# A decoder step whose first stage takes its input rows feature-major from the host: no transposes of x, and priority for the readers of the w_in products

## The chip, the cores and the metric

The kernel runs on one core of a Trainium2 chip. The metric is the device time of one execution in microseconds; the median of several runs counts. A core has five engines with a queue each: TensorE (PE, matmuls; PEld is its weight load), VectorE (DVE), ScalarE (ACT), GpSimd (POOL) and SyncE (SP), which in this kernel issues nearly all transfers.

## The reference

One inference step of a hybrid decoder layer, in float32, for a prompt of 2048 positions and a group of 8 × 8 sample positions, 1024 features:

```python
h = rmsnorm(x, g_pre_mix)
q, k, v, u = split(h @ w_in)        # 512 + 128 + 128 + 512 columns
attn = sink_attention(rope(q), rope(k), v)   # 8 heads, 2 kv heads, head_dim 64, window 128
pool = pool_mix(u)                  # trailing means over 2/4/8/16 positions, per-group map
x += rmsnorm(concat(rmsnorm(attn), rmsnorm(pool)) @ w_out)
x += rmsnorm(relu(rmsnorm(x) @ w_up)**2 @ w_down)
x += sigmoid(x @ w_ple_gate + b) * (p @ w_ple)
```

Outputs are y of both groups and the new key, value and pooling states.

## The kernel before

A product in float32 accuracy is done by `mm3` as three matmuls over values split in two: `hi` (a cast to a rounded format) and `lo` (the rest, computed by `lo_of` on VectorE). L129, L130 and L131 of the profile are these three; L125 is `lo_of`, wherever it is called from.

The program has several stages; the change lies in the first, the attention stage, up to the first matmul of w_out (its tile is `pab`, L129 and L130 in the profile), which starts at 443.44 us. After it come w_out, the two matrices of the feed-forward part (by a Strassen scheme) and the gate.

The attention stage walks over tiles of 128 positions: tile −1 is the sample (64 rows), 0 to 15 the prompt. For a tile t:

- `head(t)` issues the load of the rows `x` and of the rotary table `cs` on SP, and computes the rows' norm: ScalarE squares x into `junk` with an accumulated sum (L223), the small `rstd_of` follows, and VectorE scales `cs` with it.
- `front(t)` transposes x on TensorE in two groups of four (tile `trh`, L236, in PSUM), splits each group into `hT` (ScalarE casts, L237; VectorE subtracts, L125), and multiplies by w_in (tiles `wi`, resident in SBUF) into three PSUM tiles: `kvps` (keys and values, 24 matmuls of 256 columns), `qps` (24 of 512) and `ups` (24 of 512). The three share the two banks of the pool `mmp`. `rope` reads kvps and qps on VectorE (L258, twice L261) and adds on GpSimd (L262); the values go to `vp` (a ring of three) by two ScalarE operations and one on VectorE (L283 to L285); u goes to SBUF by ScalarE (L326). q and k are split (`qhl`, `khl`) and transposed again (`trq`, `trk`) into `qT` and `kp`. These transposes, trh and those of the attention share the two banks of the pool `tr`.
- `attention(t)`: scores `sc` (L357, L358), a fused mask and maximum on VectorE (L361, `nm`), the exponential on ScalarE (L372), the sink terms `es`, the scaling of `pr` (L387 on ScalarE, L389 on VectorE), transposes of it (`trp`, L399), their split `pt` (L401, L125), the product with the values `po` (L409, L410), and `mix` (L412, L413). `pooling(t)` works on u (L434 to L479) and has the matmuls `pq`; `finish(t)` sums squares (`pss`) and stores mix by SP to DRAM (`mixd`, L494).

The Python generators of one iteration are woven in the order that a string of letters gives (`ORDER`; f is front(t+1), a attention(t), p pooling(t), l the last finish), and the framework's scheduler then sets the order of each engine's instructions for the whole program, with each engine taking its own strictly in that order. Loads that go through `queue` keep the program's order on SP.

Towards the end of the stage w_out is loaded, and split on ScalarE (L761) and VectorE (L762) into `wo`.

Of the kernel before, what the change touches and what calls it, by code (L numbers as in the profile page):

```python
# [22 lines left out]
NS = NDEC * TDEC  # L23
# [9 lines left out]
NT = SEQ // P  # L33
# [7 lines left out]
C_HOT = C_ICNT + 64  # L41
C_COLS = C_HOT + 4

ORDER = "f f a f f l f f a f p p a f f f f a p a f f f l f a f f f"

ORDER1 = "f f f a f f f l f f a f f a f p f f f f p l f a a p a"
ORDER0 = "a f a p a p f f a a f a f a f a f p f f"


UP_N = 352  # L50
# [2 lines left out]
def tn(t):  # L53
    return NS if t < 0 else P
# [32 lines left out]
def trunk(ctx: ExitStack, tc: tile.TileContext, i: dict, o: dict):  # L87
    nc = tc.nc
    V, A, G, T, SY = nc.vector, nc.scalar, nc.gpsimd, nc.tensor, nc.sync

    xp = i["x_prompt"][0]
    xs = i["x_sample"].rearrange("b t d -> (b t) d")
    p_t = i["p_t"].rearrange("(k p) t -> p k t", p=P)
    w_in, w_out, w_up, w_down = (i[n][0] for n in ("w_in", "w_out", "w_up", "w_down"))
    w_ple, w_gate = i["w_ple"][0], i["w_ple_gate"][0]
# [3 lines left out]
    def xrows(t):  # L99
        return xs if t < 0 else xp[t * P : (t + 1) * P]  # L100
# [4 lines left out]
    ident = cp.tile([P, P], F32, name="ident")  # L105
# [14 lines left out]
    def queue(out, in_):  # L120

        tc.keep_in_program_order(SY.dma_start(out, in_))

    def lo_of(out, full, hi, eng=V):
        eng.tensor_tensor(out=out, in0=full, in1=hi.bitcast(F32), op=ALU.subtract)  # L125
# [7 lines left out]
    def rstd_of(pool, ss, n, dim, cols=1):  # L133

        r = pool.tile([P, cols], F32, tag="rst", bufs=6, name="rst")
        G.tensor_scalar(out=r[:n], in0=ss, scalar1=1.0 / dim, scalar2=EPS, op0=ALU.mult, op1=ALU.add)  # L136
        q = pool.tile([P, cols], F32, tag="rsq", bufs=6, name="rsq")
        G.tensor_tensor(out=q[:n], in0=r[:n], in1=mhalf[:n].to_broadcast([n, cols]) if cols > 1 else mhalf[:n], op=ALU.pow)
        return q


    with ExitStack() as sa:
        wp = sa.enter_context(tc.tile_pool(name="wp", bufs=1))
        fp = sa.enter_context(tc.tile_pool(name="fp", bufs=2))
# [4 lines left out]
        tr = sa.enter_context(tc.tile_pool(name="tr", bufs=2, space=PSUM))  # L149
        op = sa.enter_context(tc.tile_pool(name="op", bufs=2, space=PSUM))  # L150
# [62 lines left out]
        def head(t):  # L213

            n = tn(t)
            x = fp.tile([P, D], F32, tag="x", bufs=2, name="x")
            queue(x[:n], xrows(t))
            cs = fp.tile([P, 128], F32, tag="cs", bufs=2, name="cs")
            r0 = SEQ if t < 0 else t * P
            queue(cs[:n], i["rope"][r0 : r0 + n])  # L220
            junk = fp.tile([P, D], BF16, tag="rb", bufs=2, name="junk")
            ss = pa.tile([P, 1], F32, tag="ss", bufs=3, name="ss")
            A.activation(out=junk[:n], in_=x[:n], func=AF.Square, accum_out=ss[:n])  # L223
            rs = rstd_of(pa, ss[:n], n, D)
            V.tensor_scalar_mul(cs[:n], cs[:n], rs[:n])
            return x, cs, rs

        def front(t, x, cs, rs, res):
            n = tn(t)
            hTs = []  # L230
            for j in range(2):
                hT = fp.tile([P, 2, 4, P], F32R, tag="hT", bufs=4, name="hT")
                hTs.append(hT)
                ps = tr.tile([P, 4, P], F32, tag="tr", name="trh")
                for c in range(4):
                    T.transpose(ps[:, c, :n], x[:n, (j * 4 + c) * P : (j * 4 + c + 1) * P], ident[:n, :n])  # L236
                A.copy(out=hT[:, 0, :, :n], in_=ps[:, :, :n])  # L237
                lo_of(hT[:, 1, :, :n], ps[:, :, :n], hT[:, 0, :, :n])
                yield

            def gemm(c0, cw, ps, step=2):
                for k in range(8):
                    if k and k % step == 0:
                        yield
                    mm3(
                        ps[:n, :cw],
                        (hTs[k // 4][:, 0, k % 4, :n], hTs[k // 4][:, 1, k % 4, :n]),
                        (wi[k][:, 0, c0 : c0 + cw], wi[k][:, 1, c0 : c0 + cw]),
                        k == 0,
                        k == 7,  # L250
                    )

            def rope(ps, h, out):

                s = ps.rearrange("p (h d) -> p h d", h=h)
                b = fp.tile([P, 8, HD], F32, tag="rb", bufs=2, name="rb")[:n, :h]
                cc = cs[:n, 0:64].unsqueeze(1).to_broadcast([n, h, 64])
                V.tensor_tensor(out=out, in0=s, in1=cc, op=ALU.mult)  # L258
                for u in range(2):
                    sn = cs[:n, 64 + u * 32 : 96 + u * 32].unsqueeze(1).to_broadcast([n, h, 32])  # L260
                    V.tensor_tensor(out=b[:, :, u * 32 : u * 32 + 32], in0=s[:, :, (1 - u) * 32 : (1 - u) * 32 + 32], in1=sn, op=ALU.mult)  # L261
# [16 lines left out]
            if t >= 0:  # L278
                vp = vps[t % 3]
                vv = kvps[:, 128:256].rearrange("p (g d) -> p g d", g=2)  # L280

                hi = vp[:, 0:6].rearrange("p (a b) d -> p b a d", b=3)[:, 0]
                A.mul(out=hi, in_=vv, mul=rs)  # L283
                A.mul(out=vp[:, 4:8].rearrange("p (a b) d -> p b a d", b=2)[:, 0], in_=vv, mul=rs)
                V.scalar_tensor_tensor(out=vp[:, 1:3], in0=vv, scalar=rs, in1=hi.bitcast(F32), op0=ALU.mult, op1=ALU.subtract)  # L285
            yield
            if t >= 0:
                qps = mmp.tile([P, 512], F32, tag="mm", name="qps")
# [13 lines left out]
            if t >= 0:  # L302
                ups = mmp.tile([P, 512], F32, tag="mm", name="ups")
            for j, _ in enumerate(gemm(768, 512, ups) if t >= 0 else ()):
                yield
                if j == 0:
                    kp = over.pool.tile([P, 4, 256], F32R, tag="kp", bufs=2, name="kp")
                    ps = tr.tile([P, 4, P], F32R, tag="tr", name="trk")
# [8 lines left out]
                if j == 2:  # L317
                    qT = over.pool.tile([P, NH, P], F32R, tag="qT", bufs=1, name="qT")
                    for j in range(2):
                        ps = tr.tile([P, 4, P], F32R, tag="tr", name="trq")  # L320
# [2 lines left out]
                        A.copy(out=qT[:, 4 * j : 4 * j + 4, :], in_=ps.bitcast(F32))  # L323
                    yield
            u = pa.tile([P, 512], F32, tag="u", bufs=2, name="u")
            A.mul(out=u[:n], in_=ups[:n], mul=rs[:n])  # L326
# [4 lines left out]
            if t < 0:  # L331
                for src, dst, c in (
# [4 lines left out]
                    d = dp.tile([NS, c], F32, name="fresh")  # L337
# [261 lines left out]
        def run(*gens):  # L599
            for g in gens:  # L600
                for _ in g:
                    pass

        def weave(order, **gens):
            for c in order.split():
                next(gens[c], None)
            run(*gens.values())

        heads = {-1: head(-1)}
        load_gains(["g_pre_mix"], 0)  # L610
        for k in range(8):
            load_w_in(k)
# [33 lines left out]
    with ExitStack() as sb:  # L646
# [95 lines left out]
        with ExitStack() as s2:  # L742
# [106 lines left out]
            for tp in [0, 1, -1, 2, 3, 4, 5, 6]:  # L849
                h = []  # L850
# [543 lines left out]
```

## Time and profile before

| | |
|---|---|
| runs | 2210.32, 2214.53, 2217.34 us (median 2214.53) |
| profiled execution | 2212.33 us, its span 2210.5 us, mean granted clock 0.989 |
| PE busy, whole span | 2151.4 us (97%) |
| DVE, ACT, POOL busy | 1579.4, 957.8, 566.4 us |
| attention stage | 0 to 443.44 us |
| first kvps matmul of two tiles in steady state | 174.82 and 198.31 us |
| trh matmuls of the prompt, sum of their durations | 128 × 276 ns on average |
| `hT` casts of the prompt on ACT, subtractions on DVE | 32 × 581 ns, 32 × 685 ns |

Times are microseconds from the first instruction. In rows with starts, the first number is the start and the second the duration. A matmul's duration runs from its start to its modelled end and overlaps with the next one's; the distance between starts tells what it takes of the engine. In rows of groups the numbers behind the bar are the sum of busy time, the mean in ns, and the idle time of the engine just before them with what ended it. A row of waits gives who waited for whom, the total, how often, and the longest.

### The profile page before, as it was taken

To read this page: it belongs to the slowest core of one execution; us is meant where nothing else is said; L and a number is where in the kernel's file an instruction comes from. 1 tells how busy PE (TensorE), PEld (TensorE's weight loads), DVE (VectorE), ACT (ScalarE), POOL (GpSimd) and SP (SyncE) were. 2 spreads that over 40 slices of the span, in tenths; PEclk is the share of its full clock that TensorE was granted. 3 is DMA by queue.
4 is the path that set the end of the run, shared out by engine and by line. 5 is a ranking of instruction groups with operands and counts; after the bars stand their busy time and mean duration, and the time that the engine had idled before them with its cause. 6 is when DMAs were issued, how large, how long until landed. Compare 5 with 4: busy or idle time off the path is not lost. (4 is left out here: it accounts for less than half of the span.)

```text
span 2210.5 us, 31375 instructions
## 1 busy us (share of the span) xinstructions
PE 2151.4 (97%) x11571; PEld 1899.4 (86%) x11571; DVE 1579.4 (71%) x2716; ACT 957.8 (43%) x1856; POOL 566.4 (26%) x641
## 2 busy tenths in 40 slices
PE   8999999699989999999999999999999999999999
PEld 6888888588878999999999988788888888877887
DVE  5788888756688777655755565888888888866553
ACT  4656666634455445444644454332233232222221
POOL 2343433224340000000000045535535544300000
PEclk9999999799999999999999999999999999999999
DMA  5111110456789767766676642222321222143211
GB/s 204 51 42 43 60 43 32 135 170 194 231 249 328 238 207 256 235 193 194 204 220 197 187 122 67 89 79 68 98 89 58 89 97 85 61 150 95 82 58 39
DMA packets 288306, 295.01 MB, mean 133 GB/s; under 512 B 77654, under 2 KB 239650, under 8 KB 281977
## 3 DMA queue, kind: packets, MB, share of 16 engines
q1 hardware_dynamic: 288153, 293.01, 42.5%
q8 instruction: 91, 1.49, 0.3%
q14 instruction: 62, 0.51, 0.1%
HBM read 200.13 MB, written 94.12 MB: 133 GB/s over the span
## 5 line engine op out<-in xcount | busy, mean ns | idle before, releaser
L970 PE MATMUL up<-op,g 128*128 128x352 f32 x1344 | 434.8, 325 | 8.9 <-ACT snap L977 4.2
L971 PE MATMUL up<-op,g 128*128 128x352 f32 x1344 | 433.4, 323 | 3.0 <-DVE op L125 3.0
L972 PE MATMUL up<-op,g 128*128 128x352 f32 x1344 | 421.8, 324 | 1.0 <-DVE g L125 1.0
L1188 DVE TENSOR_TENSOR z<-dn,z 128x512 f32<-128x512 f32 x416 | 278.0, 684 | 82.3 <-PE dn L1180 73.2
L125 DVE TENSOR_TENSOR g<-raw,g 128x512 fp32r<-128x512 f32 x336 | 229.1, 700 | 89.1 <-ACT g L704 88.2
L970 PEld LDWEIGHTS up<-op,g 128*128 128x128 f32 x1344 | 253.1, 189 | 11.7 <-ACT snap L977 5.3
L971 PEld LDWEIGHTS up<-op,g 128*128 128x128 f32 x1344 | 254.8, 190 | 3.6 <-DVE op L125 3.5
L972 PEld LDWEIGHTS up<-op,g 128*128 128x128 f32 x1344 | 251.3, 189 | 1.3 <-DVE g L125 1.3
L704 ACT CAST g<-raw 128x512 fp32r<-128x512 f32 x336 | 203.4, 623 | 104.9 <-PE up L972 84.0
L1127 POOL TENSOR_TENSOR raws<-raws 128x1024 f32<-128x1024 f32 x32 | 84.1, 2640 | 620.0 <-DVE wr L125 424.9
L1178 PE MATMUL dn<-wr,ms 128*128 128x512 f32 x512 | 199.4, 390 | 0.9 <-DVE z L1188 0.9
L1179 PE MATMUL dn<-wr,ms 128*128 128x512 f32 x512 | 199.2, 389 | 0.0
L1180 PE MATMUL dn<-wr,ms 128*128 128x512 f32 x512 | 197.7, 389 | 0.0
L984 DVE TENSOR_TENSOR t<-up,snap 128x352 f32<-128x352 f32 x144 | 71.2, 520 | 118.9 <-ACT snap L977 102.3
L1178 PE MATMUL dn<-wr,m 128*128 128x512 f32 x384 | 149.5, 389 | 1.7 <-DVE z L1188 1.7
L1179 PE MATMUL dn<-wr,m 128*128 128x512 f32 x384 | 149.4, 389 | 0.0
L1180 PE MATMUL dn<-wr,m 128*128 128x512 f32 x384 | 148.9, 389 | 0.0
L704 ACT CAST m<-fr 128x512 fp32r<-128x512 f32 (+1 forms) x128 | 65.2, 513 | 187.1 <-PE dn L1180 163.3
L734 POOL TENSOR_TENSOR s<-fr 128x256 f32<-128x256 f32 x64 | 53.6, 837 | 321.6 <-DVE ms L125 221.4
L977 ACT COPY snap<-up 128x352 f32<-128x352 f32 x144 | 60.8, 454 | 167.5 <-PE up L972 167.4
L136 POOL TENSOR_SCALAR rst<-ss 128x1 f32<-128x1 f32 (+1 forms) x68 | 16.9, 249 | 390.4 <-ACT ms L680 219.9
L704 ACT CAST wr<-raws 128x1024 fp32r<-128x1024 f32 x66 | 68.7, 1050 | 107.2 <-PE dn L1180 45.8
(260 smaller groups left out, 5045.1 us busy)
## 6 DMA issues: line engine op xcount, KB each, us to landing
raw<-in_w_up_dram SPq DMA_DIRECT2D x160, 256.0 KB, 4.8
raw<-upt SPq DMA_DIRECT2D x32, 1024.0 KB, 8.0
fr<-ffd SPq DMA_DIRECT2D x64, 512.0 KB, 3.6
ffd<-r SPq DMA_DIRECT2D x96, 256.0 KB, 2.6
upt<-raw SPq DMA_DIRECT2D x16, 1024.0 KB
raws<-in_w_down_dram SPq DMA_DIRECT2D x32, 512.0 KB, 5.0
sp<-hfd SPq DMA_DIRECT2D x21, 704.0 KB, 8.5
x<-in_x_prompt_dram SPq DMA_DIRECT2D x16, 512.0 KB, 4.0
```

Of the source, the lines that this page charges most:

```text
L125: eng.tensor_tensor(out=out, in0=full, in1=hi.bitcast(F32), op=ALU.subtract)
L704: copy(out=dst[:, 0], in_=src)
L970: T.matmul(ps, l[0], r[0], start=st, stop=False, skip_group_check=not fresh)
L971: T.matmul(ps, l[0], r[1], start=False, stop=False, skip_group_check=not fresh)
L972: T.matmul(ps, l[1], r[0], start=False, stop=c == 3, skip_group_check=not fresh)
L977: A.copy(out=s, in_=ps)
L984: V.tensor_tensor(out=t, in0=ps, in1=s, op=ALU.add)
L1127: G.tensor_tensor(out=t, in0=x, in1=y, op=ALU.subtract)
L1178: T.matmul(ps, l[0], r[0], start=fresh and j == 0, stop=False, skip_group_check=not fresh)
L1179: T.matmul(ps, l[0], r[1], start=False, stop=False, skip_group_check=not fresh)
L1180: T.matmul(ps, l[1], r[0], start=False, stop=j == 1, skip_group_check=not fresh)
L1188: V.tensor_tensor(out=z, in0=ps, in1=z, op=ALU.add)
```

## The change

On the host a second copy of x, transposed (feature-major), is passed as `x_t`. `head(t)` loads from it a tile `xt` of 128 features × 8 chunks × 128 positions: 512 KB in 1024 pieces of 512 bytes (256 KB in pieces of 256 bytes for the sample). `split_head(t)` makes `hT` of it in SBUF: two ScalarE casts and two VectorE subtractions, as before, but without transposes and PSUM. x itself is still loaded, for the norm, into one buffer instead of two. The readers of PSUM behind w_in (the three VectorE operations of rope, the three of vp, and u) get priority in the scheduler. The ORDER strings lose the steps of the transposes, and split_head(t+1) is written ahead of everything else in iteration t. The cut diff:

```diff
-ORDER = "f f a f f l f f a f p p a f f f f a p a f f f l f a f f f"
+ORDER = "a f f l f f a f p p a f f f f a p a f f f l f a f f f"
...
+    x_t = i["x_t"].rearrange("(k p) t -> p k t", p=P)
...
-            x = fp.tile([P, D], F32, tag="x", bufs=2, name="x")
+            x = fp.tile([P, D], F32, tag="x", bufs=1, name="x")
             queue(x[:n], xrows(t))
+            c0 = t * P if t >= 0 else SEQ
+            xt = fp.tile([P, 8, P], F32, tag="xt", bufs=2, name="xt")
+            queue(xt[:, :, :n], x_t[:, :, c0 : c0 + n])
...
-        def front(t, x, cs, rs, res):
+        def split_head(t):
+            xt, cs, rs = heads[t]
             n = tn(t)
-            hTs = []
+            hT = fp.tile([P, 2, 8, P], F32R, tag="hT", bufs=2, name="hT")
             for j in range(2):
-                hT = fp.tile([P, 2, 4, P], F32R, tag="hT", bufs=4, name="hT")
-                hTs.append(hT)
-                ps = tr.tile([P, 4, P], F32, tag="tr", name="trh")
-                for c in range(4):
-                    T.transpose(ps[:, c, :n], x[:n, (j * 4 + c) * P : (j * 4 + c + 1) * P], ident[:n, :n])
-                A.copy(out=hT[:, 0, :, :n], in_=ps[:, :, :n])
-                lo_of(hT[:, 1, :, :n], ps[:, :, :n], hT[:, 0, :, :n])
-                yield
+                js = slice(4 * j, 4 * j + 4)
+                A.copy(out=hT[:, 0, js, :n], in_=xt[:, js, :n])
+                lo_of(hT[:, 1, js, :n], xt[:, js, :n], hT[:, 0, js, :n])
+            heads[t] = hT, cs, rs
+
+        def front(t, hT, cs, rs, res):
+            n = tn(t)
...
+                with tc.high_priority():
+                    V.tensor_tensor(out=out, in0=s, in1=cc, op=ALU.mult)
...
+                with tc.high_priority():
+                    A.mul(out=hi, in_=vv, mul=rs)
...
+            with tc.high_priority():
+                A.mul(out=u[:n], in_=ups[:n], mul=rs[:n])
...
-        heads = {-1: head(-1)}
+        heads = {}
+        heads[-1] = head(-1)
+        split_head(-1)
...
+        split_head(0)
...
+            if t + 1 < NT and t >= 0:
+                split_head(t + 1)
...
+    x_all = np.concatenate([given["x_prompt"].reshape(SEQ, D), given["x_sample"].reshape(NS, D)])
+    given["x_t"] = np.ascontiguousarray(x_all.T)
```

What this does to the engines' queues is seen at three places. On TensorE, in a steady tile of the kernel before, where the two groups of trh stand around the scores and the first w_in products of the next tile are interleaved with each other and with scores:

```order
L322 MATMUL trq<-identr,qhl 128x128 x4
L236 MATMUL trh<-ident,x 128x128 x4
L357 MATMUL sc<-kp,qT 128x256
L358 MATMUL sc<-kp,qT 128x256
...
L236 MATMUL trh<-ident,x 128x128 x4
L129 MATMUL kvps<-wi_116,hT 128x256
L130 MATMUL kvps<-wi_116,hT 128x256
L129 MATMUL qps<-wi_116,hT 128x512
L130 MATMUL qps<-wi_116,hT 128x512
L357 MATMUL sc<-kp,qT 128x256
```

and in a steady tile of the kernel after (its lines are some 9 higher), around the end of qps and the beginning of ups:

```order
L131 MATMUL qps<-wi_123,hT 128x512
...
L132 MATMUL qps<-wi_123,hT 128x512
L366 MATMUL sc<-kp,qT 128x256
L367 MATMUL sc<-kp,qT 128x256
L366 MATMUL sc<-kp,qT 128x256
L367 MATMUL sc<-kp,qT 128x256
L408 MATMUL trp<-ident,pr 128x128 x8
L130 MATMUL ups<-wi_116,hT 128x512
L131 MATMUL ups<-wi_116,hT 128x512
```

kvps, qps and ups of a tile now follow one another as blocks; between the last qps and the first ups stand four score matmuls and eight transposes. A front also runs about a tile further ahead of its attention.

On SP, a tile of the kernel before:

```order
L494 DMA mixd_79<-mix 128x1024
L122 DMA x<-in_x_prompt_dram 128x1024
L122 DMA cs<-in_rope_dram 128x128
L494 DMA mixd_80<-mix 128x1024
```

and of the kernel after:

```order
L503 DMA mixd_79<-mix 128x1024
L123 DMA x<-in_x_prompt_dram 128x1024
L123 DMA xt<-in_x_t_dram 128x8x128
L123 DMA cs<-in_rope_dram 128x128
L503 DMA mixd_80<-mix 128x1024
```

The load of xt has come in behind x, both still behind the store of mix.

On ScalarE before, where junk comes late in a tile and the hT casts follow qT, ahead of the exponentials (`pr,sm<-pr,nm`):

```order
L387 ACTIVATE pr<-pr,es 128x256 x2
L401 CAST pt<-trp 128x512 x2
L223 ACTIVATE junk,ss<-x 128x1024
...
L323 CAST qT<-trq 128x512 x2
L237 CAST hT<-trh 128x512
L416 ACTIVATE sq<-mix 128x512
L372 ACTIVATE pr,sm<-pr,nm 128x256
L237 CAST hT<-trh 128x512
```

and after:

```order
L381 ACTIVATE pr,sm<-pr,nm 128x256 x4
L391 ACTIVATE es<-es 128x4
L396 ACTIVATE pr<-pr,es 128x256 x2
L227 ACTIVATE junk,ss<-x 128x1024
L238 CAST hT<-xt 128x512 x2
L381 ACTIVATE pr,sm<-pr,nm 128x256 x2
L410 CAST pt<-trp 128x512 x2
```

junk and both hT casts now stand between the exponentials of the two halves of one tile's attention.

More of the change, by code (lines that the diff above doesn't have):

```diff
@@ L42 @@
 C_COLS = C_HOT + 4
-ORDER = "f f a f f l f f a f p p a f f f f a p a f f f l f a f f f"
-ORDER1 = "f f f a f f f l f f a f f a f p f f f f p l f a a p a"
-ORDER0 = "a f a p a p f f a a f a f a f a f p f f"
+ORDER = "a f f l f f a f p p a f f f f a p a f f f l f a f f f"
+ORDER1 = "f a f f f l f f a f f a f p f f f f p l f a a p a"
+ORDER0 = "a f a p a p a a f a f a f a f p f f"
 UP_N = 352
@@ L225, in head @@
             V.tensor_scalar_mul(cs[:n], cs[:n], rs[:n])
-            return x, cs, rs
-        def front(t, x, cs, rs, res):
+            return xt, cs, rs
+        def split_head(t):
+            xt, cs, rs = heads[t]
             n = tn(t)
-            hTs = []
+            hT = fp.tile([P, 2, 8, P], F32R, tag="hT", bufs=2, name="hT")
             for j in range(2):
-                hT = fp.tile([P, 2, 4, P], F32R, tag="hT", bufs=4, name="hT")
-                hTs.append(hT)
-                ps = tr.tile([P, 4, P], F32, tag="tr", name="trh")
-                for c in range(4):
-                    T.transpose(ps[:, c, :n], x[:n, (j * 4 + c) * P : (j * 4 + c + 1) * P], ident[:n, :n])
-                A.copy(out=hT[:, 0, :, :n], in_=ps[:, :, :n])
-                lo_of(hT[:, 1, :, :n], ps[:, :, :n], hT[:, 0, :, :n])
-                yield
+                js = slice(4 * j, 4 * j + 4)
[4 more added lines that the diff above has]
+            n = tn(t)
             def gemm(c0, cw, ps, step=2):
@@ L246, in gemm @@
                         ps[:n, :cw],
-                        (hTs[k // 4][:, 0, k % 4, :n], hTs[k // 4][:, 1, k % 4, :n]),
+                        (hT[:, 0, k, :n], hT[:, 1, k, :n]),
                         (wi[k][:, 0, c0 : c0 + cw], wi[k][:, 1, c0 : c0 + cw]),
@@ L257, in rope @@
                 cc = cs[:n, 0:64].unsqueeze(1).to_broadcast([n, h, 64])
[L258 to L261, printed above, removed]
+                with tc.high_priority():
+                    V.tensor_tensor(out=out, in0=s, in1=cc, op=ALU.mult)
+                    for u in range(2):
+                        sn = cs[:n, 64 + u * 32 : 96 + u * 32].unsqueeze(1).to_broadcast([n, h, 32])
+                        V.tensor_tensor(out=b[:, :, u * 32 : u * 32 + 32], in0=s[:, :, (1 - u) * 32 : (1 - u) * 32 + 32], in1=sn, op=ALU.mult)
                 G.tensor_tensor(out=out, in0=out, in1=b, op=ALU.add)
@@ L282, in front @@
                 hi = vp[:, 0:6].rearrange("p (a b) d -> p b a d", b=3)[:, 0]
-                A.mul(out=hi, in_=vv, mul=rs)
-                A.mul(out=vp[:, 4:8].rearrange("p (a b) d -> p b a d", b=2)[:, 0], in_=vv, mul=rs)
-                V.scalar_tensor_tensor(out=vp[:, 1:3], in0=vv, scalar=rs, in1=hi.bitcast(F32), op0=ALU.mult, op1=ALU.subtract)
+                with tc.high_priority():
+                    A.mul(out=hi, in_=vv, mul=rs)
+                with tc.high_priority():
+                    A.mul(out=vp[:, 4:8].rearrange("p (a b) d -> p b a d", b=2)[:, 0], in_=vv, mul=rs)
+                with tc.high_priority():
+                    V.scalar_tensor_tensor(out=vp[:, 1:3], in0=vv, scalar=rs, in1=hi.bitcast(F32), op0=ALU.mult, op1=ALU.subtract)
             yield
@@ L325, in front @@
             u = pa.tile([P, 512], F32, tag="u", bufs=2, name="u")
-            A.mul(out=u[:n], in_=ups[:n], mul=rs[:n])
+            with tc.high_priority():
+                A.mul(out=u[:n], in_=ups[:n], mul=rs[:n])
             if t == NT - 1:
```

## The prediction

> **What bounds the kernel now.** I read the page first, then the windows of the stage that the change touches, then single instructions.
>
> ```profile
> span 2210.5 us, 31375 instructions
> PE 2151.4 (97%) x11571; PEld 1899.4 (86%) x11571; DVE 1579.4 (71%) x2716; ACT 957.8 (43%) x1856; POOL 566.4 (26%) x641
> ...
> 110.00:165.00 55.00, 55.00 (x349) 48.69 (x348) 45.55 (x131) 33.43 (x88) 22.47 (x31) 1.00 0.13 42
> 330.00:385.00 55.00, 55.00 (x363) 48.97 (x361) 44.69 (x124) 33.37 (x86) 20.38 (x25) 1.00 0.10 32
> 385.00:443.40 58.40, 39.77 (x210) 34.07 (x209) 46.04 (x114) 37.10 (x88) 16.27 (x18) 0.73 0.41 129
> ```
>
> The window rows give the stretch, then busy time of PE, PEld, DVE, ACT and POOL, the granted clock, the DMA share and GB/s. The change lies in the attention stage, from 0 to 443.4 us (where the first matmul of w_out, pab, starts). In its steady part TensorE has no idle time at all, 55.00 of 55.00 us, while VectorE has 10 us left in 55 and ScalarE 20. So there a matmul taken away is time gained, provided that nothing new is waited for. At the stage's end it is otherwise: 39.77 us busy of 58.40 at clock 0.73.
>
> The removed transposes (trh) in one steady tile:
>
> ```profile
> 173.05 0.62 PE L236 MATMUL trh<-ident,x 128*128 128x128 f32 x4
> 173.43 0.37 PE L357 MATMUL sc<-kp,qT 128*128 128x256 f32 x1
> 173.64 0.28 PE L358 MATMUL sc<-kp,qT 128*128 128x256 f32 x1
> 173.75 0.28 PE L357 MATMUL sc<-kp,qT 128*128 128x256 f32 x1
> ...
> 174.47 0.60 PE L236 MATMUL trh<-ident,x 128*128 128x128 f32 x4
> 174.82 0.36 PE L129 MATMUL kvps<-wi,hT 128*128 128x256 f32 x1
> ...
> 198.31 0.36 PE L129 MATMUL kvps<-wi,hT 128*128 128x256 f32 x1
> ```
>
> The second column is a pipelined duration; what an operation costs is the distance between starts. Two groups of four take 173.43 − 173.05 = 0.38 and 174.82 − 174.47 = 0.35 us: 0.73 us of a tile whose period, from one first kvps matmul to the next, is 198.31 − 174.82 = 23.49 us.
>
> **The change, part by part.**
>
> Transposes: 16 prompt tiles × 0.73 = 11.7, and about 0.3 for the half-height sample tile: **−12.0 us** of TensorE time. The switch from one kind of matmul to another costs some 0.09 beside (173.43 to 173.64 is 0.21, the next distance 0.11); with two switches a tile the most it can give is 12.0 + 17 × 2 × 0.09 = 15.
>
> The other instructions of the front, in the windows 110 to 385 us (busy time, mean ns, then idle time before it):
>
> ```profile
> L361 DVE CUSTOM_DVE_ANT_0 pr<-sc,ct,nsink 128x256 f32<-128x256 f32 x88 | 38.4, 477 | 0.4
> L125 DVE TENSOR_TENSOR hT<-trh,hT 128x512 fp32r<-128x512 f32 x22 | 15.1, 685 | 0.0
> L237 ACT CAST hT<-trh 128x512 fp32r<-128x512 f32 x22 | 12.8, 581 | 0.0
> L125 DVE TENSOR_TENSOR qhl<-qr,qhl 128x512 fp32r<-128x512 f32 x12 | 8.3, 692 | 0.4
> L261 DVE TENSOR_TENSOR rb<-qps,cs 128x256 f32<-128x256 f32 x24 | 8.9, 414 | 0.0
> L258 DVE TENSOR_TENSOR qr<-qps,cs 128x512 f32<-128x512 f32 x12 | 8.2, 682 | 0.0
> L323 ACT CAST qT<-trq 128x512 fp32r<-128x512 f32 x24 | 14.3, 598 | 6.3 <-PE trq L322 6.3
> L409 PE MATMUL po<-pt,vp 128*128 128x512 f32 x48 | 19.7, 411 | 0.0
> ```
>
> The split itself stays two ACT casts (581 ns) and two DVE subtractions (685 ns) a tile; only their source moves from PSUM to SBUF. The nearest subtraction of that shape out of SBUF is qhl, 692 ns: 7 ns more each, at nothing, since VectorE has 10 us in 55 free. Freeing two PSUM banks from trh is also at nothing: PE never waited for them in steady state.
>
> Order of matmuls: the parts of a front are no longer interleaved one by one; all of qps comes before the first ups matmul. ups and kvps share two PSUM banks with qps, so the first ups waits until rope has read qps. Rope is L258 and twice L261, 0.68 + 2 × 0.41 = 1.5 us, and up to two L361 operations (0.41 us apart by their starts, below) may stand before it: 2.3. Between the last qps and the first ups TensorE has four score matmuls and eight transposes, 4 × 0.12 + 8 × 0.09 = 1.2 to 1.4 us. That leaves a **new wait** of up to 0.9 us, and 0.1 if rope goes ahead of both L361. The scores likewise stand right behind the second cast of qT (598 ns), with about 0.35 us of other work between: up to 0.2 more. Bounds 0 and 1.1 us a tile; below nothing is excluded, since before there is no idle time left to take. The priority makes rope early, so I take a little under the middle, 0.45, × 13 steady tiles = **+5.9 us** (0 to 14).
>
> Loads: the new transfer of 512 KB (1024 pieces of 512 B) a tile stands on SP behind mixd and x:
>
> ```profile
> x<-in_x_prompt_dram SPq DMA_DIRECT2D x16, 512.0 KB, 4.0
> sv<-in_state_v_dram SPq DMA_DIRECT2D x1, 512.0 KB, 7.0
> ```
>
> (the last number is us from issue to landing). The window in which sv flew, and one tile's DVE, SP and ACT rows:
>
> ```profile
> 20.90:27.90 7.00, 7.00 (x41) 5.01 (x42) 6.03 (x9) 4.37 (x5) 1.06 (x2) 1.00 1.06 313
> ```
>
> ```profile
> 197.16 0.69 DVE L413 TENSOR_TENSOR mix<-po,part 64x512 f32<-64x512 f32 x1
> 197.88 0.48 DVE L361 CUSTOM_DVE_ANT_0 pr<-sc,ct,nsink 128x256 f32<-128x256 f32 x1
> ...
> 198.29 0.48 DVE L361 CUSTOM_DVE_ANT_0 pr<-sc,ct,nsink 128x256 f32<-128x256 f32 x1
> ```
>
> ```profile
> 197.92 0.33 SPq L494 DMA_DIRECT2D mixd<-mix  x1
> 198.59 0.33 SPq L122 DMA_DIRECT2D x<-in_x_prompt_dram  x1
> ```
>
> ```profile
> 202.82 0.91 ACT L387 ACTIVATE pr<-pr,es 128x256 f32<-128x256 f32 x2
> ...
> 209.63 1.08 ACT L223 ACTIVATE junk<-x 128x1024 bf16<-128x1024 f32 x1
> ```
>
> Issues stand 0.67 us apart, so xt goes out about 199.3 in this tile's clock. Before, x had until 209.63 for junk. In the changed order junk and the two hT casts follow the first half's pr operations, which end at 203.7; hT then stands at 203.7 + 1.2 = 204.9. The deadline is 204.9 − 199.3 = **5.6 us after issue**. With x's 4.0 the transfer is in time, with sv's 7.0 (the same size and pieces) it is 1.4 late, and ScalarE stands still in front of the second half's exponentials. sv flew while the DMA engines were full (share 1.06 in its window), the steady windows show 0.10 to 0.13; so I take it in time, **0**, and keep 1.4 × 13 = +18 as the other end. The Trainium skill ("DMA: Bandwidth & Descriptors", section "Anatomy of one DMA") fits a transfer, on the GpSimd path, as 2.0 us plus its bytes at 436 GB/s: an estimate of 3.2 us, which would hide it likewise; no run here shows xt itself.
>
> Start: the sample's x in the new form, 256 KB, enters the queue ahead of w_in, whose loads ScalarE waits for.
>
> ```profile
> 8.00:18.00 10.00, 8.98 (x36) 5.33 (x36) 6.13 (x4) 4.57 (x5) 0.00 (x0) 1.00 0.92 373
> ```
>
> ```profile
> ACT wi L190 <- DMA raw<-in_w_in_dram: 6.4, 7, 4.9
> ```
>
> At 373 GB/s it takes 0.7 us; its 256 B pieces may double that. The first w_in products wait for it in full: **+1.3** (0 to 2).
>
> End of the stage: one front's matmuls more come before the first attention tile, and tiles 14 and 15 run without any beside them.
>
> ```profile
> PE trp L399 <- DVE pr L389: 9.4, 1, 9.4
> PE pq L129 <- DVE rr L472: 4.3, 1, 4.3
> PE pq L130 <- DVE rr L125: 2.5, 1, 2.5
> ```
>
> and in the groups of 385 to 443.5 us:
>
> ```profile
> L762 DVE SCALAR_TENSOR_TENSOR wo<-raw,gains,wo 128x512 fp32r<-128x512 f32 x16 | 14.3, 918 | 0.0
> ...
> L409 PE MATMUL po<-pt,vp 128*128 128x512 f32 x8 | 5.0, 622 | 0.6 <-DVE ss L491 0.3 <-ACT pt L401 0.2
> ```
>
> Those three waits, 16 us, are softmax and pooling of tile 15 behind the splitting of w_out on VectorE (14.3 us). The changed order puts about half of the wo rows between tile 14's and 15's softmax, so they would cover less of the longest wait (a gain of up to 4); tile 14 loses its cover (a loss of up to 6, the size of one such wait). Between these I take **0**.
>
> Sum: −12.0 + 5.9 + 0 + 1.3 + 0 = −4.8. The profiled execution took 2212.3 us (span 2210.5 and 1.8 around it), the median of the runs is 2214.5, 2.2 above. Against the median the forecast is 2214.5 − 4.8 = 2209.7, rounded to **2209**. What follows the stage is unchanged in kind and only starts earlier.
>
> **Rivals.**
>
> 1. The whole gain arrives. For it: TensorE is the only full engine, and rope has priority. Against: the coarse order of qps and ups. Waits 0 and the end 4 us shorter: 2214.5 − 12.0 + 1.3 − 4 = 2200; with the switches 2197.
>
> 2. The new transfer is late (the other side). Mechanism as above, on SP behind mixd and in front of the second half's exponentials. It decides from 5.6 us after issue on, and pays its lateness each tile, because mix, whose end lets SP issue the next loads, is itself late by it. 7.0 us gives 2209.7 + 18 = 2228; it turns the sign from about 6.0. For it: sv's 7.0, and that x stands ahead of it in the same queue; against: the idle DMA of the steady windows.
>
> 3. The end is longer. With two tiles without cover, gaps like the 4.3 and 9.4 appear twice, and po matmuls last 622 ns there against 411 in the steady part. Tile 14's attention is 16 sc matmuls at 0.12, 28 transposes at 0.09, 8 po at twice sc's (twice the columns) and 12 pq at about sc's: 1.9 + 2.5 + 1.9 + 1.4 = 7.7 us. At half the clock that doubles, and a wait of 4 comes with it: 2209.7 + 7.7 + 4 = 2221. It decides if PE is idle for 4 us in tile 14. The Trainium skill ("TensorE: Matmul & The Clock Gate", Part 1) says that an idle window of about 3.4 us halves the clock; the rows here agree, 4.3 us before the slow matmuls.
>
> 4. No change: the fronts are so spread that something else, the rope of the next tile or ScalarE, sets the same 23.5 us a tile. 2214. Against it: ScalarE's 20 free us in 55.
>
> **How the numbers follow.** About 0.3% (6.6 us) is what a measurement here can tell from no change: below 2208 counts as faster, above 2221 as slower. The forecast case (waits between 0.2 and 0.8 us a tile, 2206 to 2214) has 0.42, of which 0.18 lies below 2208 and 0.24 within. Rival 1 has 0.22, all faster. Rival 2 has 0.18, all slower. Rival 3 has 0.11, 0.08 of it slower and 0.03 within. Rival 4 has 0.07: 0.05 within, 0.02 slower if ScalarE falls behind. Faster 0.40, same 0.32, slower 0.28. The range leaves out the far halves of rivals 1 and 2: 2195 to 2231. The forecast's own range is 2203 to 2217.
>
> **What would show it.** Right: no trh, tile periods of 22.9 to 23.3 us, a wait of PE for DVE rb of under 0.8 us at ups, x and xt landing within 5.6 us, stage end near 438 us. Wrong: waits of ACT hT for DMA xt in every tile (rival 2), a steady tile of 22.7 without waits (rival 1), a window of low clock over 35 us long at the stage's end (rival 3), or a changed span behind pab, which I hold to be untouched.

## The result: 1.5% slower, and the profile after

The changed kernel takes 2245.45 us (median of 4 runs, 2239.48 to 2248.53) against 2213.24 of the kernel before in the same session: a ratio of 1.0146, with a 95% interval of 1.0125 to 1.0166, some 32 us more. The forecast was 2209, with a range of 2195 to 2231, so the time lies above it and the direction is wrong.

The loss lies in the attention stage alone. In the two profiled executions (2212.3 and 2247.8 us, 35.5 apart) its end, the first w_out matmul, comes at 478.51 us instead of 443.44, 35.1 later; from there to the end it is 1767.4 us against 1767.1. The windows after (columns as before):

```profile
span 2245.9 us, 31110 instructions
```

```profile
110.00:165.00 55.00, 49.31 (x286) 41.72 (x287) 40.78 (x112) 30.34 (x79) 20.60 (x28) 0.97 0.27 81
...
330.00:385.00 55.00, 51.34 (x320) 45.14 (x320) 46.32 (x127) 34.30 (x90) 20.53 (x26) 1.00 0.23 72
385.00:443.40 58.40, 45.41 (x267) 38.87 (x265) 47.69 (x136) 37.46 (x100) 18.67 (x25) 0.89 0.31 98
```

TensorE, which stood at 55.00 of 55.00 us before, is now idle for 4 to 6 us in each of the steady windows. What it waits for, from 0 to 480 us (total, times, longest):

```profile
PE ups L130 <- DVE rb L266: 18.1, 11, 2.4
PE po L418 <- ACT pt L410: 8.7, 6, 3.5
...
PE sc L366 <- DVE nm L370: 4.6, 4, 1.6
...
PE ups L130 <- DVE vp L293: 2.7, 1, 2.7
```

The first row is one wait in almost every tile. A steady tile runs from one first kvps matmul to the next; the wait stands between the eight trp and the first ups:

```profile
275.37 0.36 PE L130 MATMUL kvps<-wi,hT 128*128 128x256 f32 x1
...
288.87 1.04 PE L408 MATMUL trp<-ident,pr 128*128 128x128 f32 x8
291.62 0.47 PE L130 MATMUL ups<-wi,hT 128*128 128x512 f32 x1 [1.71 <-DVE rb L266]
...
300.20 0.36 PE L130 MATMUL kvps<-wi,hT 128*128 128x256 f32 x1
```

The period is 300.20 − 275.37 = 24.83 us, against 23.5 before. VectorE in that stretch shows why rope is late:

```profile
288.19 0.75 DVE L398 TENSOR_SCALAR pr<-pr,es 128x256 f32<-128x256 f32 x2
288.86 0.34 DVE L266 TENSOR_TENSOR rb<-kvps,cs 128x64 f32<-128x64 f32 x2
289.12 0.28 DVE L468 SCALAR_TENSOR_TENSOR r<-us,ux 128x128 f32<-128x128 f32 x1
289.32 0.47 DVE L370 CUSTOM_DVE_ANT_0 pr<-sc,ct,nsink 128x256 f32<-128x256 f32 x1
...
289.72 0.47 DVE L370 CUSTOM_DVE_ANT_0 pr<-sc,ct,nsink 128x256 f32<-128x256 f32 x1
...
290.13 0.68 DVE L263 TENSOR_TENSOR qr<-qps,cs 128x512 f32<-128x512 f32 x1
290.73 0.74 DVE L266 TENSOR_TENSOR rb<-qps,cs 128x256 f32<-128x256 f32 x2
```

The last qps matmul starts at 288.17, but the rope of it (L263) only at 290.13: the end of pr, the rope of kvps, a pooling operation and two score operations stand ahead. Rope ends at 291.47, and ups starts 0.15 us later. The second half of the rope of kvps (`rb`, 288.86) is itself late: that product was ready at 279, when VectorE began to read it, and its bank was held for ten microseconds, to 289.20. The other readers did not hold it: ScalarE read it at 279.07 and 279.97, and VectorE made its part of `vp` at 280.50. The 2.26 us that ScalarE stands still before 279.07 end with po and a value tile, at about the moment at which kvps is ready too. DVE, then ACT:

```profile
279.19 0.29 DVE L263 TENSOR_TENSOR kr<-kvps,cs 128x128 f32<-128x128 f32 x1 [1.25 <-PE kvps L132]
```

```profile
279.07 0.37 ACT L289 ACTIVATE vp<-kvps,rsq 128x128 fp32r<-128x128 f32 x1 [2.26 <-PE po L418]
```

In the kernel before, both halves of that rope stand side by side, and the first ups starts before the rope of qps does, so it cannot have had the bank of qps. DVE, then PE:

```profile
276.83 0.28 DVE L258 TENSOR_TENSOR kr<-kvps,cs 128x128 f32<-128x128 f32 x1
277.03 0.34 DVE L261 TENSOR_TENSOR rb<-kvps,cs 128x64 f32<-128x64 f32 x2
...
281.44 0.68 DVE L258 TENSOR_TENSOR qr<-qps,cs 128x512 f32<-128x512 f32 x1
```

```profile
279.62 0.39 PE L129 MATMUL ups<-wi,hT 128*128 128x512 f32 x1
```

After, ups waits for the end of the rope of qps, though the bank of kvps was free by 289.20, before the transposes ended (289.91). So ups was given the bank of qps when the order was made, and not by what was free at that moment. No view shows which bank a tile has; this is inferred from what ups waits for. No idle time of VectorE stands before the late `rb`: it is late by its place in the order.

Where the 35.1 us come from can be counted on TensorE: each matmul at the median distance to its successor that its group has in the kernel before; distances that exceed it by over 0.3 us are waits; the rest of the excess is mostly matmuls at half clock. In us, before and after:

| stretch | work | waits | slow matmuls |
|---|---|---|---|
| start to the first half's scores of tile 0 (56.2; 72.0) | 40.4; 46.7 | 7.3; 10.0 | 3.8; 9.3 |
| to those of tile 4 (150.8; 182.6) | 91.9; 96.8 | 1.4; 9.1 | 1.3; 4.8 |
| to those of tile 13 (362.4; 406.2) | 211.7; 203.8 | 0.0; 17.3 | −0.1; 2.5 |
| to the end of the stage (443.4; 478.5) | 53.5; 35.4 | 21.6; 27.8 | 5.9; 9.0 |
| sum | 397.5; 382.7 | 30.3; 64.2 | 10.9; 25.6 |

The first matmul comes 1.4 us later. Work −14.8, waits +33.9, slow matmuls +14.7 and these 1.4 make 35.2. (Work in the start is larger because the front runs ahead, and smaller at the end for the same reason.) The work is a count: its fall of 14.8 us is the 136 transposes at their median distance of 0.109 us. By their own distances in a steady tile, 0.73 us as the prediction read them, it would be the 12.0 of the forecast.

### The profile page after: what moved, and what is told of

It is laid out like the page before. It is cut to its first block, busy times and chain, and to the rows that moved or that the text cites. A ratio compares the mean times of both kernels' runs of the same rounds, so it can differ in the third digit from the quotient of the medians.

```text
span 2245.9 us, 31110 instructions
## 1 busy us (share of the span) xinstructions
PE 2159.6 (96%) x11435; PEld 1899.8 (85%) x11435; DVE 1594.3 (71%) x2716; ACT 961.6 (43%) x1856; POOL 566.2 (25%) x641
## 5 line engine op out<-in xcount | busy, mean ns | idle before, releaser
L1192 PEld LDWEIGHTS dn<-wr,ms 128*128 128x128 f32 x512 | 96.2, 188 | 22.1 <-issue 1.2
```

Of the source, the lines that this page charges most:

```text
L1192: T.matmul(ps, l[0], r[0], start=fresh and j == 0, stop=False, skip_group_check=not fresh)
```

## Experiments

All ratios are to the kernel before on the same chip, with 95% intervals; the changed kernel's is 1.0146 (1.0125 to 1.0166). "First scores" are the last of the first half's scores of tile 0.

**Is it the priority?** The changed kernel without it, and the kernel before with it alone.

```diff
-                with tc.high_priority():
-                    V.tensor_tensor(out=out, in0=s, in1=cc, op=ALU.mult)
+                V.tensor_tensor(out=out, in0=s, in1=cc, op=ALU.mult)
```

(and the other four places; the second kernel adds the same five to the kernel before.)

> The changed kernel without the priority of the readers behind w_in. Theory A (removing the transposes lets the whole front run a tile ahead; its kvps then holds a PSUM bank because the ring of three value tiles is full, and ups has to wait for rope of qps): the order of the matmuls stays in blocks, so the tile period stays between 24.5 and 25.5 us and the time between 2240 and 2260. Theory B (the priority disturbs VectorE's order): the time falls to 2205 to 2220.

> The kernel before, with its transposes, plus the priority. Theory A: no loss, the fronts stay interleaved, 2205 to 2220. Theory B: most of the loss, 2230 or more.

Without priority 2258.2 us, 1.0202 (1.0178 to 1.0226), slower still; priority alone 2217.7, 1.002 (1.0008 to 1.0033), a little slower than before. Both times are as forecast for the case that the priority does no harm. The priority is not what costs; in the changed kernel it is worth 13 us. What it is worth shows in two tiles without priority:

```profile
266.62 0.47 PE L130 MATMUL ups<-wi,hT 128*128 128x512 f32 x1 [1.91 <-DVE rb L265]
...
268.11 0.63 PE L130 MATMUL ups<-wi,hT 128*128 128x512 f32 x1
268.53 0.63 PE L131 MATMUL ups<-wi,hT 128*128 128x512 f32 x1
```

```profile
293.26 0.47 PE L130 MATMUL ups<-wi,hT 128*128 128x512 f32 x1 [1.92 <-DVE rb L265]
...
294.71 0.39 PE L130 MATMUL ups<-wi,hT 128*128 128x512 f32 x1
```

The wait is 0.2 us longer than with priority, and behind it the matmuls run at half speed for about 3.4 us (0.43 us apart) in five of eight steady tiles, as in the first of the two fences, and not in the others, as in the second; with priority (1.71 us idle) in none. Those tiles have periods of 26.6 instead of 25.0. What tells the five from the three is where the wait falls (columns as before; the granted clock is the third number from the end):

```profile
264.62:268.03 3.41, 1.50 (x7) 1.23 (x7) 3.41 (x11) 3.41 (x11) 2.46 (x4) 1.00 0.00 0
268.03:271.44 3.41, 3.41 (x9) 2.64 (x9) 3.41 (x10) 1.14 (x5) 0.00 (x0) 0.50 0.00 0
```

```profile
288.51:291.92 3.41, 2.83 (x21) 2.43 (x19) 3.07 (x13) 2.45 (x6) 2.10 (x5) 1.00 0.55 158
291.92:295.33 3.41, 2.07 (x9) 1.78 (x10) 3.41 (x11) 3.41 (x11) 2.27 (x3) 1.00 0.00 0
295.33:298.75 3.42, 3.42 (x16) 2.83 (x16) 3.38 (x10) 0.67 (x4) 0.00 (x0) 1.00 0.00 0
```

In every trace of this case the granted clock changes only at times that lie whole multiples of 3.413 us apart. In the five tiles the 1.9 us lie inside one such step, and the next step has half the clock; in the three they lie across the end of a step.

**Is it the depth of a ring?** kvps is emptied late. Two candidates hold it: the ring of three value tiles, whose oldest is still read by the attention (the 2.26 us above end with it), and the two buffers of the rope scratch.

```diff
-        for r in range(3):
+        for r in range(4):
```

(with the indices modulo 4), and, by itself:

```diff
-            b = fp.tile([P, 8, HD], F32, tag="rb", bufs=2, name="rb")[:n, :h]
+            b = fp.tile([P, 8, HD], F32, tag="rb", bufs=3, name="rb")[:n, :h]
```

> The changed kernel with four value tiles vp instead of three, nothing else. Theory A: kvps is emptied before the attention that reads the oldest value tile is done, ups finds a free bank, the wait of PE for DVE rb (16 us in ten tiles) falls to under 4, the tile period to 22.6 to 23.6 us; time 2205 to 2228. Theory C (the load of xt comes late and sets the period): no change, 2238 to 2250.

> The changed kernel with three buffers of the rope scratch rb (shared with junk) instead of two; the vp ring stays at three. Theory A with the ring as its cause: no change, 2240 to 2250, period 24.8. If the scratch buffer is what holds kvps's bank (its last reader is rb at the end): the time falls by 10 to 25 us, as with the ring.

Three scratch buffers change little: 2239.6, 1.0117 (1.0092 to 1.0142), period 24.84, and `rb` of kvps is still ten microseconds late (`kr` at 271.77, `rb` at 281.43). Four value tiles were to win back most of the loss; the kernel takes 2306.1, 1.0421 (1.0399 to 1.0443), with periods of 30.2 to 33.2 us. The waits with four value tiles:

```profile
PE trp L408 <- DVE pr L398: 31.4, 9, 5.3
PE ups L130 <- DVE rb L266: 19.3, 8, 5.2
PE sc L366 <- DVE nm L370: 14.9, 15, 2.6
```

That theory, in this form, fell. With a deeper ring the scheduler lets the front run further ahead still: in a tile of this run qps begins (273.68) before trk and trq (278.49), which stand ahead of it in the changed kernel, and the waits grow. The ring did not cause the loss.

**Is it that nothing holds the front back?** In the scheduler's order the kernel before has the products of w_in interleaved with scores and with each other; the changed one has them in blocks, with and without priority. What it lacks is the transposes. So a part of them was put back as a gate, where they stood, with the rest of x from xt. With this the split is back at its old place (and the ORDER strings with it), and x has two buffers again:

```diff
+            ps = tr.tile([P, 4, P], F32, tag="tr", name="trh")
+            T.transpose(ps[:, 0, :n], x[:n, 0:P], ident[:n, :n])
+            A.copy(out=hT[:, 0, :1, :n], in_=ps[:, :1, :n])
...
+            A.copy(out=hT[:, 0, 1:4, :n], in_=xt[:, 1:4, :n])
```

> The changed kernel, but the first of the eight 128-column chunks of x is transposed on TensorE again (one matmul into the pool tr, then split from PSUM) and the other seven are split from xt, at the place where the transposes stood; x has two buffers again. Theory D (the transposes, besides their work, held the front back until the attention before it let go of the banks; without them it runs a tile ahead and holds a PSUM bank too long): the scheduler's order puts kvps behind the scores again, ups takes the bank of kvps and waits for nothing; tile period 22.7 to 23.4 us, wait of PE ups for DVE rb under 2 us in all, time 2198 to 2214. Theory E (the new load, or splitting from SBUF, is what costs): 2235 to 2250, as the changed kernel.

> As the run with one chunk, with four chunks transposed and four from xt. Theory D: tile period 0.25 to 0.4 us longer than with one, 23.0 to 23.7; time 2203 to 2217. Theory E: half of the loss, 2228 to 2240.

> As the run with one chunk transposed, without the priority. Theory D: the priority mattered only where banks were short, so within 8 us of the run with it (2198 to 2220). If the priority is worth by itself what it was worth without the gate (13 us): 2212 to 2227.

One chunk: 2222.8, 1.0046 (1.0028 to 1.0063). Four: 2226.9, 1.0062 (1.0042 to 1.0082). One without priority: 2222.9, 1.0042 (1.0024 to 1.0059). So 22.7 of the 32 us come back with one transposed chunk and the split at its old place (1.00% of the 1.46%), the wait for rope is not among TensorE's waits any more, and with it gone the priority is worth nothing (0.1 us). What changed is not that the blocks are gone: with one gate 18 matmuls of qps, eight transposes and all 24 of ups still follow one another. But in the same tile `rb` of kvps comes right behind `kr` again (258.02 and 257.82), and ups starts at 263.44, before the rope of qps (263.84). So it is the bank that counts. The forecasts of time were missed all the same, by 9, 10 and 3 us: the period with one gate is 24.0 us, not 22.7 to 23.4:

```profile
253.25 0.36 PE L130 MATMUL kvps<-wi,hT 128*128 128x256 f32 x1
...
277.27 0.36 PE L130 MATMUL kvps<-wi,hT 128*128 128x256 f32 x1
```

The next pair asked whether a second gate brings the rest, and whether the loads cost anything by themselves. With two gates the first chunk of each half is transposed, as two groups, and hT is two tiles again; the second kernel is the one before, which also loads xt and never reads it.

> The changed kernel with two gates instead of one: in each of the two halves of x the first chunk is transposed on TensorE (two matmuls a tile instead of eight), the other three come from xt; hT is two tiles of four buffers as before. Theory D, sharpened (what the order loses is the fine interleaving of kvps, qps, scores and ups that the two transposes held in place): the order of the matmuls is nearly the old one, tile period 22.9 to 23.4, no wait over 0.4 us in a steady tile; 2202 to 2213. If one gate was enough and the rest of its 24.0 us has another cause: 23.8 to 24.2 and 2218 to 2226 again.

> The kernel before with all its transposes and no priority, plus the loads of xt, which nothing reads. Theory D: the loads cost only their place at the start, 0 to 3 us: 2212 to 2219. Theory E (the load costs by itself): 2225 or more.

Two gates: 2219.4, 1.0038 (1.0023 to 1.0053), with a period of 23.27 us, better than the 23.5 of before, no wait in a steady tile, and the stage's end at 444.3. The period is as forecast, the time is 6 us above the forecast. The loads alone: 2219.9, 1.0034 (1.0021 to 1.0048), with the period of before, but the first scores at 62.6 instead of 56.2. They cost 0.34%, 7.5 us, where 0 to 3 were expected. The window of 27 to 56 us in the kernel before and with the loads alone:

```profile
27.00:56.00 29.00, 28.05 (x222) 22.66 (x221) 18.73 (x64) 11.26 (x30) 10.31 (x14) 1.00 0.30 91
```

```profile
27.00:56.00 29.00, 27.61 (x205) 21.51 (x202) 16.89 (x59) 8.39 (x23) 7.79 (x11) 1.00 0.47 145
```

TensorE gets through 205 matmuls where it had 222: the loads of xt for the sample and for tiles 0 and 1 (issued at 1.4, 16.1 and 28.8 us) come into a start in which the DMA engines are full (their share before is 0.92 from 8 to 18 us and 1.05 from 18 to 27 us), and what stands behind them is late.

**Is it the start?** The same two kernels, with xt only from tile 2 on; and a third, without any transposes from tile 2 on, whose gate is a tile of the pool tr that VectorE clears by one column and copies into hT before ScalarE overwrites it.

```diff
-            xt = fp.tile([P, 8, P], F32, tag="xt", bufs=2, name="xt")
-            queue(xt[:, :, :n], x_t[:, :, c0 : c0 + n])
+            xt = None
+            if t >= 2:
+                xt = fp.tile([P, 8, P], F32, tag="xt", bufs=2, name="xt")
+                queue(xt[:, :, :n], x_t[:, :, c0 : c0 + n])
```

```diff
-                    T.transpose(ps[:, c, :n], x[:n, (j * 4 + c) * P : (j * 4 + c + 1) * P], ident[:n, :n])
+                    V.memset(ps[:, 0, 0:1], 0.0)
+                    V.tensor_copy(hT[:, 0, 0, 0:1], ps[:, 0, 0:1])
```

> The kernel before with all its transposes and no priority, plus the unused loads of xt, but only from tile 2 on (not for the sample, tile 0 and tile 1, whose loads fall into the start when the DMA engines are full). Theory F (the loss of the run with all loads lies at the start, in the 1.25 MB that go out among the loads of w_in, the states and the constants): no loss left, within 0.2% of before, 2208 to 2216, first scores near 56.2 us. If the loads cost in the steady tiles: still 0.3% slower, 2217 to 2222.

> The version with two gates (two of eight chunks transposed), with xt only from tile 2 on; the sample and tiles 0 and 1 are transposed as before. Theory F and D together: first scores near 56.2, tile period 23.27, stage end 438 to 441; 2206 to 2213. If the start is not the loads: 2216 to 2223 as with two gates.

> From tile 2 on no transposes at all: the gate is a tile of the pool tr of which VectorE clears one column and copies it into hT before ScalarE writes it; xt only from tile 2 on; priority kept. Theory D (the front has to be held back, by whatever means): no waits of PE for rope, tile period 22.7 to 23.3 us, 2200 to 2212, the fastest of all. If the position of the transposes in TensorE's own order is what interleaves the products: period 23.5 or more, 2213 to 2225.

The late loads alone cost nothing: 2213.9, 1.0005 (0.9996 to 1.0014). In steady tiles of this kernel a further 512 KB a tile, which nothing reads, costs no time that can be seen. Two gates with late loads: 2211.9, 0.9996 (0.9987 to 1.0005), the same as before; its stage ends at 440.9 us, 2.5 earlier, too little to be told from no change. The gate without TensorE: 2235.9, 1.0109 (1.0095 to 1.0124), with a period of 25.4 us, slower than both forecasts, so "by whatever means" was wrong. Its waits:

```profile
PE sc L375 <- DVE nm L379: 6.9, 14, 1.4
...
PE po L427 <- ACT pt L419: 3.2, 10, 0.3
PE trk L328 <- DVE pt L126: 3.1, 10, 0.3
...
PE tru L455 <- DVE trh L247: 2.6, 10, 0.3
```

No long one is left in a steady tile; there are several short ones. The last row is the gate itself, which the transposes of u (tru) wait for. The run differs from the one with two gates and late loads only in the gate and in the two chunks of a tile that go through PSUM there, and it is 24.0 us slower. So a gate on VectorE does not do what the two transposes do. A possible reason is that the transposes, where they stood in TensorE's own order, also set what stands beside what; that is argued, not shown, and kvps and qps are interleaved in this run too. The split's old place was not run by itself. Here it comes with the gate on VectorE, and both together are some 0.2% better than the changed kernel with late loads (below).

**Is it the start in the changed kernel too, and is the wait of ups a shortage of banks?** The changed kernel with xt from tile 2 on (in steady state its order is unchanged), and with a third bank for the products of w_in, once taken from the scores, once from the transposes.

```diff
-        mmp = sa.enter_context(tc.tile_pool(name="mmp", bufs=2, space=PSUM))
-        scp = sa.enter_context(tc.tile_pool(name="scp", bufs=2, space=PSUM))
+        mmp = sa.enter_context(tc.tile_pool(name="mmp", bufs=3, space=PSUM))
+        scp = sa.enter_context(tc.tile_pool(name="scp", bufs=1, space=PSUM))
```

> The changed kernel with xt only from tile 2 on; the sample and tiles 0 and 1 are transposed as before. In steady state the order of matmuls is that of the changed kernel. If the start is the loads (theory F): first scores 4 to 9 us earlier than the changed kernel's 72.0, period still 24.8, 2232 to 2241. If the start is the front that runs ahead: first scores as late, 2242 to 2250.

> The changed kernel with three PSUM banks for kvps, qps and ups and one for the scores (before: two and two). If ups waits for a bank: its wait for rope of qps falls from 18 us to under 3, and the tile period to 23.0 to 24.0 unless the scores wait for their one bank instead; 2215 to 2235. If ups waits for something else: the wait stays, 2240 to 2255.

> The changed kernel with three PSUM banks for kvps, qps and ups and one for all transposes (before: two and two). If ups waits for a bank: the wait for rope of qps is gone, but each group of transposes waits for the copy of the one before, at ten groups a tile of 0.3 to 0.6 us: period 24 to 27, 2230 to 2280. If the wait is for something else it stays beside these: 2260 or more.

Late loads: 2242.8, 1.0126 (1.0107 to 1.0145), so 2.6 us better than the changed kernel, within its spread and 2 us above the forecast; the first scores come at 63.3 instead of 72.0, but of these 8.6 us only 4.8 are left at the stage's end (473.7). Where the rest went, probably to the fronts that still run ahead, is not shown. A third bank taken from the scores: 2292.1, 1.0358 (1.0336 to 1.038); taken from the transposes: 2356.7, 1.0645 (1.0626 to 1.0663). Both are slower than forecast. But in both the wait for rope is gone from TensorE's largest waits: taken from the scores, for example, ups starts at 273.31 while the rope of its qps ends only at 281.43. So the wait was for a bank. Taken from the scores, these stand in its place:

```profile
PE sc L366 <- DVE nm L370: 20.3, 16, 2.7
PE kvps L130 <- ACT hT L238: 19.7, 11, 2.7
```

and taken from the transposes:

```profile
PE po L418 <- ACT pt L410: 29.0, 39, 6.2
PE kvps L132 <- DVE hT L126: 7.1, 3, 2.9
```

The four pools have two banks each in the changed kernel; in these two runs whoever gave one up waits in its place.

## Why the prediction was wrong

- **Transposes, −12.0 (at most −15).** Nothing speaks against it. The 14.8 us of the table are a count by medians and no measurement of what was won; with two gates the distances behind trh fell by 0.62 us a tile, six eighths of 0.73 being 0.55.
- **New wait at ups, +5.9 (0 to 14).** The right place, and the step that failed most: 17.3 us in the nine tiles from tile 4 to tile 13, 1.9 in each; the bound was 0.9, or 1.1 with the wait for qT. (By its own figures it is 2.3 − 1.2 = 1.1, or 1.3; the prediction took the longer cover of 1.4.) The step counted two score operations ahead of rope on VectorE. The rows of 288.19 to 290.13 show three more: the end of pr, the rope of kvps and a pooling operation. From the end of the last qps (288.17 + 0.39 = 288.56) to the first score operation (289.32) they take 0.8 us, and 0.9 + 0.8 is the 1.7 that TensorE stands idle. And the step took the wait as a detail of the order, where it is a sign that kvps keeps its bank for ten microseconds and that ups is given the one of qps.
- **Split from SBUF, 7 ns more a subtraction, at nothing.** Mis-sized: the subtraction for hT takes 869 ns on average from 0 to 440 us (32 of them, at most 1541), 184 more than before. In the steady tile above it stands behind rope (292.40), so it does not lengthen the wait there.
- **Loads in steady state, 0 (up to +18).** Right, by a narrow margin. The landing is 5.8 us for xt, 0.2 past the estimated deadline; but in the steady tile the casts came later than estimated, at 290.10, 6.4 us after the issue at 283.65:

```profile
x<-in_x_prompt_dram SPq DMA_DIRECT2D x16, 512.0 KB, 4.9
xt<-in_x_t_dram SPq DMA_DIRECT2D x16, 512.0 KB, 5.8
```

```profile
ACT hT L238 <- DMA xt<-in_x_t_dram: 0.4, 2, 0.2
```

ScalarE waits 0.4 us for it in all, from 110 to 385 us, so rival 2 is out, and the loads alone from tile 2 on cost nothing. The time ended on the slower side as rival 2 would have (2228), by another mechanism. The fit of the Trainium skill ("DMA: Bandwidth & Descriptors", section "Anatomy of one DMA"), which is for the GpSimd path, makes an estimate of 3.2 us of such a transfer. Here 5.8 us were measured, on SP and behind x in its queue.

- **Start, +1.3 (0 to 2).** Mis-sized: only the sample's 256 KB were counted. The two loads of tiles 0 and 1, 1 MB more, fall into the same start. The loads alone cost 6.4 us at the first scores and 8.4 us at the end of the stage, and nothing when these three are left out. The other part of the 15.8 us by which the first scores are late, 7.1 us with late loads, is the front that runs ahead, which had no term.
- **The first tiles** had no term. Between the scores of tile 0 and tile 4 waits grew by 7.7 us and slow matmuls by 3.5, before the order settled into its period. The order was read for a steady tile only.
- **End of the stage, 0 (−4 to +6).** Waits +6.2 and slow matmuls +3.1, beyond the upper end together; the direction is that of rival 3, at 9.3 us near its 11.7. That is in part luck: its signs, an idle time of 4 us and a stretch of low clock over 35 us long, are not there. The longest wait is 3.5 us (before: 9.4), and the longest stretch at half clock is 23.9 us (430.99 to 454.89). The Trainium skill ("TensorE: Matmul & The Clock Gate", Part 1) puts the limit at an idle window of about 3.4 us. In the run without priority waits of 1.9 us halved the clock in some tiles and not in others. The 4.3 us that the prediction took as agreeing do not show the limit either: TensorE is idle from 410.99, and the granted clock falls at 411.71, after 0.7 us of it; in the 3.41 us ahead of 411.71 it was idle for 2.09.
- **Tile period, 22.9 to 23.3 foretold.** It is 24.83.
- **The sum** is 2209.7, which rounds to 2210 and not to 2209; nothing hangs on it.

Two things remain open. Why the scheduler, without the transposes, puts half of the rope of kvps ten microseconds late and the products in blocks is not known; that it does, and that with one or two short transposes in the old place ups no longer waits, is shown. And of the one-gate version's period, 24.0 us, only the place is known: against before, the distances behind trh are 0.65 us shorter in a tile, those behind po 0.63 and behind trp 0.54 longer (the largest piece is 0.49, between po and trk); a second gate leaves 0.15 and 0.11 of these.

## What to carry to other kernels

When a scheduler sets the order, an instruction that is removed also removes the constraint that it was: look at what else becomes ready earlier, which buffer that then holds and until which reader, and who needs it. Before forecasting a gain from the bound engine, walk through its order at the start, in the middle and at the end, and at each wait count everything that stands ahead of the releasing instruction in its own queue. A load that costs nothing in steady state can cost in a start that is bound by transfers.

## What the runs showed of the hardware that was not expected

- An idle TensorE of 1.71 us in each of nine tiles never lowered its clock, though in four of them it lay inside one step of 3.413 us; 1.9 us lowered it in five of eight tiles, those in which it lay inside one step, for the next 3.4 us (matmuls of 512 columns 0.43 us apart instead of 0.23); 2.66 us did it at once (up to 41.69 us after the start of the changed kernel, the step's end being 41.87). A fifth of a microsecond of waiting could so cost 1.6 us, and whether it did hung on where the wait fell.
- Six of eight transposes taken away shortened a tile by 0.23 us only (23.5 to 23.27, two gates). Counted as in the table, work fell by 0.65 us a tile, and 0.4 came back in many distances between matmuls that are each less than 0.3 us longer than before (po followed by trq 0.27 instead of 0.23, trq followed by trh 0.33 instead of 0.09). A stall too short to be listed as a wait can take most of a gain.
